# A decoder step on one core: w_in read with eight neighbouring rows per partition

## The chip, the cores and the metric

The kernel runs on one NeuronCore of a Trainium2 chip. Its engines work side by side: TensorE (matrix products, and transposes as products with an identity), VectorE, ScalarE, GpSimd, and SyncE, which mainly issues DMA transfers. The core's 16 DMA engines move data between the memory outside (DRAM) and the on-chip memory SBUF, which has 128 partitions. Products are written to PSUM and evacuated from there by ScalarE and VectorE. The metric is the device time of one execution in microseconds; lower is better.

## What is computed

One layer of a hybrid recurrent decoder for 2048 prompt tokens and 64 sample tokens, width 1024. The part that matters here is its beginning: the normalised input is multiplied by one wide matrix, and the product is cut into the inputs of all branches.

```python
IN_SPLITS = (LRU_WIDTH, LRU_WIDTH, GDN_QKV_W, GDN_VAL_W, GDN_HEADS, GDN_HEADS, D_MODEL, D_MODEL)
IN_WIDTH = sum(IN_SPLITS)                      # 8208
...
u = rms_norm(x, norm_pre)                      # x * rsqrt(mean(x*x) + eps) * norm_pre
z = jnp.einsum('btd,de->bte', u, w_in)         # w_in is (1024, 8208), float32
lru_x, lru_gate, gdn_qkv, gdn_gate, gdn_b, gdn_a, m_lru, m_gdn = jnp.split(z, offsets, axis=-1)
```

Behind it follow causal convolutions, a gated linear recurrence, a gated delta rule in chunks with its triangular inverses, two branch projections (w_br_lru, w_br_gdn), a gated merge and the output product (w_out). The sum over d in the product above has 1024 terms; in which order they are taken changes nothing but rounding.

## The kernel before

The prompt is worked through in four blocks of 512 tokens (`blkno` 0 to 3); block 1 also carries the 64 sample tokens. The contraction index of an input product has 1024 values; it is dealt out as eight tiles of 128 partitions. Both operands must have the same deal: partition p of tile k holds row k * 128 + p of w_in, and the transposed input holds the same index there.

**Weights.** `worder` is the list of all weight tiles in the order in which the products need them. In block 0 `wraw_of` loads a raw tile from DRAM through SyncE's queue: mostly 256 columns of w_in for all 1024 rows (1 MB; 128 columns in two cases), into `raw` of [128, 8, 256]. One row of w_in is 8208 floats or 32,832 bytes long, so each of the 1024 rows gives one contiguous piece of 1 KB. Tiles of the branch matrices are loaded by the same lines; their rows are 4 KB long. `split` then makes two tiles of it, high and low part (ScalarE writes the high part, GpSimd the low), in a buffer `whl` of which there are three. `wstore` writes both to DRAM (`dW`, 1 MB, contiguous); a buffer is free again when its store has landed and its products are done. From block 1 on `wfetch` reads `dW` back and w_in is not touched any more.

**Input.** `u_load` brings x into `ux` tiles (tokens on partitions), `u_norm` scales each token, and `u_tile(xh, k)` transposes the columns of tile k on TensorE (four tokens' tiles into one PSUM bank, five in block 1), where ScalarE and VectorE write high and low part, scaled by `npre[:, k]`, the norm's gains for the 128 rows of tile k. In a transpose the input tile is what TensorE loads as weights and the identity is what streams past. Block 0 does all eight tiles at the start; for the other blocks they are done during the output product of the block before. `npre` itself is loaded as eight rows of 128 (`r0`), transposed on TensorE and copied by VectorE.

**Order.** TensorE's order is that of the program; a small scheduler (`Weave`) interleaves side tasks between the products by estimated times. The other engines' orders come from the tile framework. All loads of weights, their stores and most other transfers go through SyncE's queue.

Of the kernel before, what the change touches and what calls it, by code (L numbers as in the profile page):

```python
# [22 lines left out]
F32 = mybir.dt.float32  # L23
# [47 lines left out]
C_LRUX, C_LRUG, C_Q, C_K, C_V, C_GG, C_B, C_ML, C_MG = 0, 1024, 2048, 3072, 4096, 5120, 6144, 6160, 7184  # L71
# [83 lines left out]
def body(ctx, tc, x_prompt, x_sample, state_lru_conv, state_lru_h, state_gdn_conv, state_gdn_S,  # L155
# [5 lines left out]
    V, T, SP = nc.vector, nc.tensor, nc.sync  # L161
    A, G = Ordered(tc, nc.scalar), nc.gpsimd

    win = w_in[0]
# [15 lines left out]
    def act(out, in_, func=AF.Copy, **kw):  # L180
        A.activation(out, in_, func, **kw)

    def gtile():
        t = pg.tile([128, 512], F32, name="g", tag="g")
        return t
# [8 lines left out]
    def tr(out, in_, idn):  # L194
        T.transpose(out, in_, idn)  # L195
        W.pe(TR)
# [33 lines left out]
    dW = [dram.tile([128, 2, 1024], F32, name=f"dW{i}") for i in range(len(wplace))]  # L230
    wstored, wstores, wraws = set(), [], {}

    def wraw_of(n):

        e = worder[n]
        if key(e) not in wraws:
            src, c = e
            if isinstance(c, tuple):
                raw = rp.tile([128, 4, 256], F32, name="raw", tag="raw")
                SP.dma_start(raw, src[c[1] * 512:(c[1] + 1) * 512, c[0] * 256:(c[0] + 1) * 256]  # L240
                             .rearrange("(k p) c -> p k c", p=128))
                wraws[key(e)] = raw
            else:
                two = [key(x) for x in worder[n:n + 7]].count((src.tensor.name, c + 128))
                w = 128 + 128 * two
                raw = rp.tile([128, 8, w], F32, name="raw", tag="raw")
                SP.dma_start(raw, src[:, c:c + w].rearrange("(k p) c -> p k c", p=128))
                for j in range(1 + two):
                    wraws[src.tensor.name, c + 128 * j] = raw[:, :, 128 * j:128 * j + 128]
        return wraws[key(e)]  # L250
# [44 lines left out]
    ident = const.tile([128, 128], F32, name="ident")  # L295
# [11 lines left out]
    npre = const.tile([128, 8], F32, name="npre")  # L307

    def u_load(bn, pool):
        nt = NCH + (1 if bn == SB else 0)  # L310
        xh = []
        for i in range(nt):
            m = 128 if i < NCH else NS
            xt = pool.tile([128, D], F32, name=f"ux{i}")
            SP.dma_start(xt[:m], xp[bn * TB + i * 128: bn * TB + (i + 1) * 128] if i < NCH else xs)
            xh.append((xt, m))
        return xh
# [14 lines left out]
    def u_tile(xh, k):  # L332
        hi = pA.tile([128, TB + NS], F32R, name="a", tag="a")
        lo = pA.tile([128, TB + NS], F32R, name="a", tag="a")
        for gi, grp in enumerate([xh[:4]] + ([xh[4:]] if len(xh) > 4 else [])):
            t = gtile()
            n = 0
            for xt, m in grp:
                tr(t[:, n:n + m], xt[:m, k * 128:(k + 1) * 128], ident[:m, :m])
                n += m  # L340
            cs = slice(gi * 512, gi * 512 + n)
            act(hi[:, cs], t[:, :n], AF.Copy, scale=npre[:, k:k + 1])
            V.scalar_tensor_tensor(out=lo[:, cs], in0=t[:, :n], scalar=npre[:, k:k + 1],
                                   in1=hi[:, cs].bitcast(F32), op0=OP.mult, op1=OP.subtract)
        return hi, lo
# [45 lines left out]
    with tc.tile_pool(name="init", bufs=2, side="right") as ip:  # L391
        rows = lambda a: a.rearrange("o (g p) -> (o g) p", p=128)
        with tc.tile_pool(name="u0", bufs=1) as up:
            r0 = ip.tile([8, 128], F32, name="r0")
            SP.dma_start(r0, rows(norm_pre))
            xh = u_load(0, up)
            t = gtile()
            tr(t[:, :8], r0, ident[:8, :8])
            V.tensor_copy(npre, t[:, :8])
            wraw = ip.tile([128, 8, 16], F32, name="wraw", bufs=1)  # L400
            SP.dma_start(wraw, win[:, C_B:C_B + 16].rearrange("(k p) c -> p k c", p=128))
            u_norm(xh, up)
            zz = ip.tile([128, 96], F32, name="zz", bufs=1)
            V.memset(zz, 0.0)
            V.tensor_copy(wst[:, 256:352], zz)
            V.tensor_copy(wst3[:, :, 0:16], wraw)
            V.tensor_tensor(out=wst3[:, :, 16:32], in0=wraw, in1=wst3[:, :, 0:16].bitcast(F32), op=OP.subtract)
            wfetch(2)
            r1 = ip.tile([128, 128], F32, name="r1")
            SP.dma_start(r1[8:40], lru_conv_w[0].rearrange("w (g p) -> (w g) p", p=128))  # L410
            SP.dma_start(r1[40:48], rows(lru_conv_b))
            SP.dma_start(r1[48:56], rows(lru_ba))
            SP.dma_start(r1[56:64], rows(lru_bx))
            SP.dma_start(r1[64:72], rows(lru_a_logit))
            SP.dma_start(r1[72:73], gdn_norm_w)
            SP.dma_start(r1[0:8], rows(norm_pre))
            r2 = ip.tile([128, 128], F32, name="r2")
            SP.dma_start(r2[:96], gdn_conv_w[0].rearrange("w (g p) -> (w g) p", p=128))
            SP.dma_start(dtb, bass.AP(tensor=gdn_dt_bias.tensor, offset=gdn_dt_bias.offset, ap=[[0, 128], [1, 8]]))
            SP.dma_start(negA, bass.AP(tensor=gdn_A_log.tensor, offset=gdn_A_log.offset, ap=[[0, 128], [1, 8]]))  # L420
            u = [u_tile(xh, k) for k in range(8)]
            t = gtile()
            tr(t[:, :73], r1[:73], ident[:73, :73])
            V.tensor_copy(par, t[:, :73])
        G.affine_select(out=tri, in_=ones, pattern=[[1, 128]], compare_op=OP.is_ge, fill=0.0,
                        base=0, channel_multiplier=-1)
        G.affine_select(out=offm.rearrange("p (a b) -> p a b", b=32), in_=ones.rearrange("p (a b) -> p a b", b=32),
                        pattern=[[-32, 4], [0, 32]], compare_op=OP.is_ge, fill=0.0, base=-32,
                        channel_multiplier=1)
        V.tensor_scalar(offm, offm, -1.0, None, op0=OP.mult)  # L430

        blk = const.tile([64, 64], F32, name="blk")
        blk3 = blk.rearrange("p (a b) -> p a b", b=8)
        G.affine_select(out=blk3, in_=ones[:64, :64].rearrange("p (a b) -> p a b", b=8),
                        pattern=[[-8, 8], [0, 8]], compare_op=OP.is_ge, fill=0.0, base=0, channel_multiplier=1)
        G.affine_select(out=blk3, in_=blk3, pattern=[[8, 8], [0, 8]], compare_op=OP.is_ge, fill=0.0,
                        base=7, channel_multiplier=-1)
        tris = const.tile([64, 64], F32, name="tris")
        V.tensor_tensor(out=tris, in0=blk, in1=tri[:64, :64], op=OP.mult)
        negs = const.tile([64, 64], F32, name="negs")  # L440
        V.tensor_scalar(negs, tris, 1.0, BIG, op0=OP.subtract, op1=OP.mult)
        bsel = blk3[:, :, 0]
        G.memset(halog, 0.0)
        G.memset(halol, 0.0)
        G.memset(hlast, 0.0)
        t = gtile()
        tr(t[:, :96], r2[:96], ident[:96, :96])
        V.tensor_copy(cwg.rearrange("p w g -> p (w g)"), t[:, :96])
        V.tensor_scalar(hba, par[:, 48:64], 0.5, None, op0=OP.mult)
        lp = ip.tile([128, 8], F32, name="lp")  # L450
        log1pexp_neg_abs(ip, lp, lal, [128, 8])
        V.scalar_tensor_tensor(out=ls4[:, 0:8], in0=lal, scalar=0.0, in1=lp, op0=OP.min, op1=OP.subtract)
        V.tensor_scalar(ls4[:, 0:8], ls4[:, 0:8], 4.0, None, op0=OP.mult)
        V.tensor_scalar(ls4[:, 8:16], ls4[:, 0:8], -1.0, None, op0=OP.mult)
        tc.keep_in_program_order(A.activation(negA, negA, AF.Exp))
        V.tensor_scalar(negA, negA, -1.0, None, op0=OP.mult)
# [52 lines left out]
    for blkno in range(NBLK):  # L509
# [402 lines left out]
        for g in range(8):  # L912
# [3 lines left out]
            raw = kl.tile([128, 2, 128], F32, name="gwr", tag="er", bufs=2)  # L916
# [324 lines left out]
        for q in range(4):  # L1241
# [11 lines left out]
            for i, k in order:  # L1253
                c0, m = ntok[i]
                r0 = 128 - m
# [19 lines left out]
        for i, (c0, m) in enumerate(ntok):  # L1275
            r0 = 128 - m
# [42 lines left out]
```

## Time and profile before

| | |
|---|---|
| Median of three runs | 2709.49 us (2701.82 to 2710.34) |
| Profiled execution | 2704.15 us, its span 2702.4 us |
| TensorE busy | 2576.4 us (95% of the span) |
| VectorE, ScalarE, GpSimd busy | 56%, 33%, 21% |
| Queue of SyncE and ScalarE (q1) | 295162 packets, 553.57 MB, 65.1% of 16 engines' span |
| Issues of w_in loads | 31 of 1024 KB, 2 of 512 KB |
| Mean granted clock of TensorE | 0.984 |

A share of the span is an average over stages with different limits. The rows below therefore cut block 0 (about the first 700 us) into stages. A window of the DMA view says how many packets began in it, how many MB they moved, and what share of the 16 engines' time in the window they took; share times 16 times the window's length, divided by packets, is the mean time of one packet.

### The profile page before, as it was taken

To read this page: it belongs to the slowest core of one execution; us is meant where nothing else is said; L and a number is where in the kernel's file an instruction comes from. 1 tells how busy PE (TensorE), PEld (TensorE's weight loads), DVE (VectorE), ACT (ScalarE), POOL (GpSimd) and SP (SyncE) were. 2 spreads that over 40 slices of the span, in tenths; PEclk is the share of its full clock that TensorE was granted. 3 is DMA by queue.
4 is the path that set the end of the run, shared out by engine and by line. 5 is a ranking of instruction groups with operands and counts; after the bars stand their busy time and mean duration, and the time that the engine had idled before them with its cause. 6 is when DMAs were issued, how large, how long until landed. Compare 5 with 4: busy or idle time off the path is not lost.

```text
span 2702.4 us, 39930 instructions
## 1 busy us (share of the span) xinstructions
PE 2576.4 (95%) x15332; PEld 2234.1 (83%) x15332; DVE 1515.1 (56%) x3449; ACT 880.1 (33%) x1708; POOL 561.2 (21%) x444
## 2 busy tenths in 40 slices
PE   7777898889999999999999999999999999999999
PEld 5656677778899999998999788888889788888888
DVE  4557677753455767777423557566523457566522
ACT  4225533332432452333203225333302235333301
POOL 3433522336212011000210211100110111110200
PEclk9898899999999999999999999999999999999999
DMA  8998976878877656544465787554467786655465
GB/s 241 262 271 193 270 226 166 178 235 316 304 249 255 193 180 193 162 154 134 171 216 219 252 271 227 199 175 156 156 241 257 252 280 215 206 170 168 160 238 199
DMA packets 309177, 581.82 MB, mean 215 GB/s; under 512 B 70561, under 2 KB 218042, under 8 KB 263930
## 3 DMA queue, kind: packets, MB, share of 16 engines
q1 hardware_dynamic: 295162, 553.57, 65.1%
q10 hardware_dynamic: 13824, 25.70, 2.5%
q8 instruction: 121, 1.98, 0.3%
q14 instruction: 70, 0.57, 0.1%
HBM read 421.61 MB, written 157.59 MB: 214 GB/s over the span
## 4 chain that ended last, share of the span: by engine, by line
PE 78%; DMA 7%; DVE 6%; issue 3%; ACT 2%; POOL 2%; SPq 1%; ACTq 0%; POOLq 0%; DVEq 0%
PE mm L533 19%; PE mm L531 18%; PE mm L529 18%; PE g L191 8%; PE c L191 5%; DMA dW<-whl 3%; PE g L195 3%; DVE cvy L560 2%; PE mm L1264 2%; PE mm L1266 2%; PE mm L1262 2%; DMA er<-dgc 1%; POOL whl L204 1%; DMA dgc<-gr 1%; DMA raw<-in_w_in_dram 1%
## 5 line engine op out<-in xcount | busy, mean ns | idle before, releaser
L533 PE MATMUL mm<-a,whl 128*128 128x512 f32 (+2 forms) x2288 | 840.3, 367 | 11.4 <-POOL whl L204 11.4
L529 PE MATMUL mm<-a,whl 128*128 128x512 f32 (+2 forms) x2288 | 835.4, 365 | 13.6 <-ACT whl L143 6.4
L531 PE MATMUL mm<-a,whl 128*128 128x512 f32 (+2 forms) x2288 | 835.6, 365 | 0.0
L533 PEld LDWEIGHTS mm<-a,whl 128*128 128x128 f32 x2288 | 436.9, 191 | 70.7 <-POOL whl L204 14.1
L529 PEld LDWEIGHTS mm<-a,whl 128*128 128x128 f32 x2288 | 436.8, 191 | 69.5 <-ACT whl L143 7.6
L531 PEld LDWEIGHTS mm<-a,whl 128*128 128x128 f32 x2288 | 436.2, 191 | 51.8
L560 DVE SCALAR_TENSOR_TENSOR cvy<-cvr,cwg,cvy 128x512 f32<-128x512 f32 x288 | 263.2, 914 | 19.1 <-ACT cvy L143 13.5
L204 POOL TENSOR_TENSOR whl<-raw,whl 128x1024 fp32r<-128x1024 f32 x80 | 200.4, 2507 | 255.9 <-ACT whl L143 243.8
L533 PE MATMUL mm<-a,whx 128*128 128x512 f32 (+2 forms) x592 | 210.1, 355 | 0.0
L531 PE MATMUL mm<-a,whx 128*128 128x512 f32 (+2 forms) x592 | 209.6, 354 | 0.0
L529 PE MATMUL mm<-a,whx 128*128 128x512 f32 (+2 forms) x592 | 208.3, 352 | 0.0
L1200 DVE SCALAR_TENSOR_TENSOR pt<-tm,mm 128x512 f32<-128x512 f32 (+1 forms) x80 | 47.3, 593 | 188.7 <-PE mm L533 188.7
L143 ACT ACTIVATE cvr<-mm 128x512 f32<-128x512 f32 (+1 forms) x160 | 81.6, 510 | 185.2 <-PE mm L533 178.7
L143 ACT ACTIVATE whl<-raw 128x1024 fp32r<-128x1024 f32 x88 | 93.0, 1057 | 146.9 <-DMA dW<-whl 88.6
L1055 POOL TENSOR_TENSOR st<-st,mhalf 128x4 f32<-128x4 f32 x32 | 32.2, 1007 | 513.8 <-DVE st L1053 383.8
L143 ACT ACTIVATE th<-cvy 128x512 f32<-128x512 f32 (+1 forms) x96 | 61.9, 645 | 203.6 <-DVE cvy L560 158.3
L1266 PE MATMUL mm<-whl,bt 128*128 128x256 f32 x440 | 123.8, 281 | 0.8 <-DVE yss L1240 0.8
L1262 PE MATMUL mm<-whl,bt 128*128 128x256 f32 x440 | 123.9, 282 | 0.2 <-ACT bt L143 0.2
L1264 PE MATMUL mm<-whl,bt 128*128 128x256 f32 x440 | 124.0, 282 | 0.0
L533 PEld LDWEIGHTS mm<-a,whx 128*128 128x128 f32 x592 | 112.0, 189 | 13.8 <-issue 1.5
L529 PEld LDWEIGHTS mm<-a,whx 128*128 128x128 f32 x592 | 111.8, 189 | 12.0
L531 PEld LDWEIGHTS mm<-a,whx 128*128 128x128 f32 x592 | 111.7, 189 | 11.9
(328 smaller groups left out, 4511.2 us busy)
## 6 DMA issues: line engine op xcount, KB each, us to landing
whl<-dW SPq DMA_DIRECT2D x199, 1024.0 KB
dW<-whl SPq DMA_DIRECT2D x88, 1024.0 KB
whx<-dW SPq DMA_DIRECT2D x65, 1024.0 KB
raw<-in_w_in_dram SPq DMA_DIRECT2D x31, 1024.0 KB
dtm<-tmo ACTq DMA_DIRECT2D x48, 256.0 KB
tm<-dtm SPq DMA_DIRECT2D x48, 256.0 KB
ux<-in_x_prompt_dram SPq DMA_DIRECT2D x16, 512.0 KB
er<-dgc SPq DMA_DIRECT2D x32, 256.0 KB
```

The lines of the kernel that those rows point to most:

```text
L143: r = f(*args, **kw)
L191: T.matmul(out, a, b, start=start, stop=stop)
L195: T.transpose(out, in_, idn)
L204: (eng or G).tensor_tensor(out=lo, in0=src, in1=hi.bitcast(F32), op=OP.subtract)
L529: T.matmul(ps[:, :n], wh, mh[:, c0:c0 + n], start=k == 0, stop=False)
L531: T.matmul(ps[:, :n], wh, ml[:, c0:c0 + n], start=False, stop=False)
L533: T.matmul(ps[:, :n], lo[:, k, :], mh[:, c0:c0 + n], start=False, stop=k == 7)
L560: V.scalar_tensor_tensor(out=y[:, :TB], in0=raw[:, i:i + TB], scalar=cw[:, i, ti:ti + 1], in1=y[:, :TB], op0=OP.mult, op1=OP.add)
L1200: proj(mov, lambda ps, c0, n: V.scalar_tensor_tensor(out=t_[:, c0:c0 + n], in0=x[:, c0:c0 + n], scalar=1.0, in1=ps[:, :n], op0=OP.add, op1 ...
L1262: T.matmul(ps[:, :256], mh[:, cs], wh[:, k % 4], start=k == 0, stop=False)
L1264: T.matmul(ps[:, :256], mh[:, cs], wl[:, k % 4], start=False, stop=False)
L1266: T.matmul(ps[:, :256], ml[:, cs], wh[:, k % 4], start=False, stop=k == 7)
```

## The change

Partition p of an input product now holds rows 8p to 8p + 7 of w_in, and tile k is the k-th of each eight. Three places follow it: the loads of w_in (`krows`, used by `wraw_of` for tiles of w_in alone and by the small gate load `wraw`), the transposes of the input, which take every eighth column of x, and `npre`, which in this deal is a plain reshape of norm_pre and is loaded directly.

```diff
+    def krows(a, by8):
+
+        return a.rearrange("(p k) c -> p k c", k=8) if by8 else a.rearrange("(k p) c -> p k c", p=128)
+
     def wraw_of(n):
...
-                SP.dma_start(raw, src[:, c:c + w].rearrange("(k p) c -> p k c", p=128))
+                SP.dma_start(raw, krows(src[:, c:c + w], src is win))
...
-                tr(t[:, n:n + m], xt[:m, k * 128:(k + 1) * 128], ident[:m, :m])
+                tr(t[:, n:n + m], xt[:m].rearrange("t (p k) -> t k p", k=8)[:, k], ident[:m, :m])
...
-            r0 = ip.tile([8, 128], F32, name="r0")
-            SP.dma_start(r0, rows(norm_pre))
+            SP.dma_start(npre, norm_pre.rearrange("o (p k) -> (o p) k", k=8))
             xh = u_load(0, up)
-            t = gtile()
-            tr(t[:, :8], r0, ident[:8, :8])
-            V.tensor_copy(npre, t[:, :8])
             wraw = ip.tile([128, 8, 16], F32, name="wraw", bufs=1)
-            SP.dma_start(wraw, win[:, C_B:C_B + 16].rearrange("(k p) c -> p k c", p=128))
+            SP.dma_start(wraw, krows(win[:, C_B:C_B + 16], True))
```

The order of instructions changes at the start alone. TensorE's first instructions before (r is the tile r0, ux a tile of x, g a PSUM bank):

```order
L195 MATMUL g<-ident,r_208 128x8
L195 MATMUL g<-ident,ux_210 128x128
L195 MATMUL g<-ident,ux_212 128x128
L195 MATMUL g<-ident,ux_214 128x128
L195 MATMUL g<-ident,ux_216 128x128
```

and now:

```order
L195 MATMUL g<-ident,ux_209 128x128
L195 MATMUL g<-ident,ux_211 128x128
L195 MATMUL g<-ident,ux_213 128x128
L195 MATMUL g<-ident,ux_215 128x128
L195 MATMUL g<-ident,ux_209 128x128
```

The transpose of r0 is gone (and with it VectorE's copy into npre); the rest follows in the same order. SyncE's queue begins before with these transfers:

```order
L395 DMA r_208<-in_norm_pre_dram 8x128
L315 DMA ux_210<-in_x_prompt_dram 128x1024
L315 DMA ux_212<-in_x_prompt_dram 128x1024
L315 DMA ux_214<-in_x_prompt_dram 128x1024
L315 DMA ux_216<-in_x_prompt_dram 128x1024
L401 DMA wraw<-in_w_in_dram 128x8x16
L247 DMA raw<-in_w_in_dram 128x8x256 x2
```

and now:

```order
L398 DMA npre<-in_norm_pre_dram 128x8
L319 DMA ux_209<-in_x_prompt_dram 128x1024
L319 DMA ux_211<-in_x_prompt_dram 128x1024
L319 DMA ux_213<-in_x_prompt_dram 128x1024
L319 DMA ux_215<-in_x_prompt_dram 128x1024
L401 DMA wraw<-in_w_in_dram 128x8x16
L251 DMA raw<-in_w_in_dram 128x8x256 x2
```

The first transfer goes to all 128 partitions; nothing else moved in the queue, here or later.

## Rows read from the trace of the kernel before

**Rows 1.** Page, 40 slices of the span: DMA engines' busy share in tenths.
```profile
DMA  8998976878877656544465787554467786655465
```
**Rows 2.** Windows: stretch, us, busy (instructions) by engine, PEclk, DMA share, GB/s.
```profile
96.00:360.00 264.00, 209.69 (x866) 165.62 (x865) 164.49 (x270) 103.50 (x148) 108.63 (x64) 0.89 0.93 246
360.00:600.00 240.00, 215.19 (x1258) 175.71 (x1257) 170.12 (x303) 83.42 (x158) 74.70 (x38) 0.97 0.73 192
600.00:690.00 90.00, 89.46 (x394) 72.80 (x393) 33.91 (x32) 27.91 (x36) 58.80 (x31) 1.00 0.86 310
```
**Rows 3.** Chain of waits from 30 to 360 us, longest pieces: start, us, what.
```profile
96.77 17.89 DMA dW<-whl
123.79 7.22 DMA dW<-whl
146.28 9.44 DMA er<-dgc
178.31 9.85 DMA dW<-whl
256.93 21.65 DMA dW<-whl
...
314.33 17.17 DMA dW<-whl
```
**Rows 4.** Timeline of SyncE's queue: start, us of the issue, line, transfer.
```profile
95.46 1.21 SPq L247 DMA_DIRECT2D raw<-in_w_in_dram  x1
...
246.94 0.43 SPq L247 DMA_DIRECT2D raw<-in_w_in_dram  x1
...
298.15 1.00 SPq L247 DMA_DIRECT2D raw<-in_w_in_dram  x1
```
**Rows 5.** DMA view, 516 to 519 us (stores alone): packets, MB, share of 16 engines.
```profile
q1 hardware_dynamic: 127, 1.04, 83.9%
```
**Rows 6.** DMA view, 602 to 605.4 us: a load of w_br.
```profile
q1 hardware_dynamic: 1055, 1.06, 92.4%
```
**Rows 7.** DMA view, 464.3 to 476.6 us: a load of w_in.
```profile
q1 hardware_dynamic: 1063, 1.26, 101.6%
```
**Rows 8.** DMA view, 397.6 to 404.7 us: a load of w_in.
```profile
q1 hardware_dynamic: 1107, 1.62, 94.0%
```
**Rows 9.** DMA view, 98.1 to 110.5 us: a load of w_in.
```profile
q1 hardware_dynamic: 1156, 1.52, 102.4%
```
**Rows 10.** DMA view, 212 to 226 us: a load of w_in.
```profile
q1 hardware_dynamic: 1371, 2.28, 99.5%
```
**Rows 11.** DMA view, 250 to 260 us: most of a load of w_in.
```profile
q1 hardware_dynamic: 819, 0.90, 98.3%
```
**Rows 12.** DMA view, issues from 30 to 360 us: count, KB each.
```profile
raw<-in_w_in_dram SPq DMA_DIRECT2D x19, 1024.0 KB
```
**Rows 13.** Chain of waits from 360 to 600 us, shares by line.
```profile
by line: issue 21.3%; DVE cvy L560 12.9%; PE c L191 9.3%; PE g L191 7.5%; POOL whl L204 7.0%; PE mm L533 6.2%; PE mm L531 5.5%; PE mm L529 5.2%; ACT cvy L143 3.2%; PE g L195 2.9%; POOL st L1055 2.5%; ACT whl L143 2.4%; DVE R L977 2.0%; DVE 
```
**Rows 14.** Timeline of ScalarE at the start: start, us, instruction [idle before <-releaser].
```profile
19.09 1.06 ACT L143 ACTIVATE whl<-raw 128x1024 fp32r<-128x1024 f32 x1 [3.59 <-DMA raw<-in_w_in_dram]
20.05 1.83 ACT L143 ACTIVATE a<-g,npre 128x512 fp32r<-128x512 f32 x3
```
**Rows 15.** Instructions on the ux tiles: count, ns min/median/max, first and last start, forms.
```profile
L195 PEld LDWEIGHTS g<-ident,ux x136: 134/141/231, 7.7 to 2069.9; 128*128 128x128 f32 x128, 64*128 64x128 f32 x8
L195 PE MATMUL g<-ident,ux x136: 243/272/477, 7.7 to 2070.0; 128*128 128x128 f32 x128, 64*128 64x64 f32 x8
...
L330 DVE TENSOR_SCALAR ux<-ux,urr x9: 746/753/764, 6.8 to 2052.5; 128x1024 f32<-128x1024 f32 x8, 64x1024 f32<-64x1024 f32 x1
```
**Rows 16.** The same view of line 797, a copy with permuted axes.
```profile
L797 DVE COPY invTT<-invT x4: 1119/1134/1141, 236.9 to 2265.2; 128x1024 f32<-128x1024 f32 x4
```
**Rows 17.** DMA view, 11.7 to 15.3 us: the first load of w_in.
```profile
q1 hardware_dynamic: 1144, 1.05, 91.7%
```

## The prediction, written before the result

> **What bounds the kernel now.** I read the page's slices first: the DMA engines are nearly full in the first slices, about 0.8 to 0.9 busy through slice 7, and looser after that [rows 1]. The change touches the loads of w_in, and these are issued in block 0 alone (later blocks read the split copies back from dW). So I cut block 0 into stages [rows 2]. [...] From 360 to 600 the DMA share is 0.73, and from 600 to 690 TensorE is full (89.46 of 90 us, clock 1.00). Only the first of the three is a stage where DMA decides.
>
> The chain of waits says the same [rows 3]. Between 30 and 360 us its longest pieces are stores of split weights (dW<-whl) and one broadcast (er<-dgc): 17.89, 7.22, 9.44, 9.85, 21.65 and 17.17 us, together 83.2 us. A store of 1 MB that has the DMA engines to itself takes 3 us [rows 5], so these wait in the queue. What is ahead of them stands in SyncE's list [rows 4]: some microseconds before each of the six pieces a load of w_in was issued (before the first at 95.46 us, before the fifth at 246.94, before the last at 298.15). A store must land before its whl buffer is free (three of them), and ScalarE's next split waits for that.
>
> **The price of a w_in load.** I take windows filled by one load and turn the share of 16 engines into time per packet. A load of 1 MB is 1024 packets of 1 KB (1.05 MB). Pure stores: 0.839 x 16 x 3 us = 40.3 us for 1.04 MB, 38.7 us per MB [rows 5]. A load of w_br, which has the same shape but rows 4 KB apart: 0.924 x 16 x 3.4 = 50.3 us for 1055 packets, 48 ns each [rows 6]. A w_in load alone at 464 us: 1.016 x 16 x 12.3 = 199.9 us, less 0.21 MB of stores (8.1), is 192 us for 1024 packets, 187 ns each [rows 7]. Another at 397 us: 106.8 less 0.57 MB (22.1) is 84.7 us, 83 ns each [rows 8]. So w_in's packets cost two to four times w_br's, at the same size, beside the same kind of stores. The difference is where the rows lie: w_in's rows are 8208 x 4 = 32,832 bytes apart, and in the order "(k p)" the eight pieces of a partition are 128 rows, 4.2 MB, apart.
>
> I call loads near 187 ns costly. Three more are at 98 us (203.2 less 18.2 for 0.47 MB, 181 ns) [rows 9], at 212 us (222.9 less 47.6 for 1.23 MB, 171 ns) [rows 10] and at 250 us (157.3 us for 819 packets, 192 ns) [rows 11]. Of the 19 full loads from 30 to 360 us [rows 12] these three are costly, and the other 16 I put at the 83 ns of [rows 8].
>
> **The change, part by part.**
>
> *The loads of w_in (the main term).* Same number of packets, same 1 KB. The eight pieces of a partition now are neighbouring rows, 32,832 bytes apart, and a partition starts 262,656 bytes after the one before. No row of the trace shows this pattern. The lower bound of its price is w_br's 49 ns (rounded up), the upper the 187 ns of the costly loads. I take 55 ns, near the lower end: w_br's regular step from row to row is fast, and the costly pattern is the one whose consecutive pieces jump by megabytes. Then a costly load gives back (187 - 55) x 1024 / 16 ns = 8.4 us of all engines, another (83 - 55) x 64 ns = 1.8 us, and all from 30 to 360 us 3 x 8.4 + 16 x 1.8 = 54 us (62 at 49 ns).
>
> How much lies on the path? At least what the chain shows: the pieces at 96.77 and 256.93 stand behind a costly load (2 x 8.4), the other four behind one of the rest (4 x 1.8): 24 us. At most all 54 (or 62), because at a share of 0.93 each transfer queues behind the one before. TensorE then limits: its 209.69 busy us in 264, less what the clock of 0.89 cost, leave room for at least 54 us. Once it is fed, VectorE's and GpSimd's work between the products stands next in the chain, so I don't take all: 42. After 360 us I take nothing: DMA is 0.73 busy there and the chain names VectorE, TensorE and "issue" but neither raw nor dW [rows 13].
>
> *The start.* ScalarE idles 3.59 us for the first raw tile at 19.09 us, with the evacuations of the input's transposes queued behind it; the next one begins at 20.05 [rows 14]. A faster load gives 0 to 3.6; I take 2.
>
> *npre.* Gone: one transpose and one copy, both in idle time at the start. New: SyncE's first DMA has 128 pieces of 32 bytes, not 8 of 512. Its first reader is ScalarE's evacuation at 20.05 us, and it is the first DMA of the kernel; behind it in SyncE's queue stand the loads of x, which could start a fraction of a microsecond later. Cost 0; without that cover it would be one small DMA's latency. The small load wraw keeps its 1024 pieces and is first read by products that come after all transposes.
>
> *The transposes.* Their input is read with a step of 8 elements, by the weight load. Now the load takes 141 ns (median of 136) under a matmul of 272 ns [rows 15], so it may grow to 272 ns for nothing. The nearest strided rows are VectorE's: a permuted copy of 128x1024 takes 1134 ns, a plain pass over as many elements 753 [rows 15, 16], a factor of 1.5, or 212 ns here. Cost 0 in a row of transposes, some 0.1 us at the first of each group; I take 1 us in all. The order of instructions on every engine is otherwise the same, so no new wait arises.
>
> Sum: 2704.15 - 42 - 2 + 1 = 2661 us against the profiled execution (span 2702.4). The three runs have a median of 2709.49, 5.3 above that execution, and spread over 8.5 us; the median of the changed kernel should stand between 2661 and 2666. I give 2663.
>
> **The rivals.**
>
> *Nothing changes.* The same 1024 rows are read in another order. If some columns of w_in simply lie badly (all on few parts of the memory), the order can't help: 2704 to 2709 us. For it: the load at 464 us is costly from end to end, while the first load, with the same order of rows, ran at 0.917 x 16 x 3.6 = 52.8 us for 1144 packets, 46 ns [rows 17]; so columns matter. Against it: that a pattern with the same rows can reach 46 ns also shows that these rows are not costly by themselves. [...] Chance 0.17.
>
> *Slower: the new order collides.* All 16 DMA engines now walk neighbouring rows, and if they meet on the same part of the memory, every load runs at the 187 ns of [rows 7]. The 16 others from 30 to 360 us then cost (187 - 83) x 64 = 6.7 us more each, 107 us; with the same part on the path as above (42 of 54) 83 us, and some 10 after 360 us: 2797 us. It decides from a mean of (3 x 187 + 16 x 83) / 19 = 99 ns per packet of w_in. Against it: w_br's loads walk rows at a regular step too and don't collide. Chance 0.11.
>
> *The strided transposes set the pace.* [...] Chance 0.06.
>
> **How the numbers follow.** A measurement of this kernel tells 0.3% (8 us) from no change. Forecast 0.66, its own range 2636 (62 + 3.6 us) to 2690 (half of the excess stays and little of it is on the path). Nothing changes 0.17 and strided transposes 0.06 end within 0.3%; slower 0.11. So faster 0.66, same 0.23, slower 0.11. The range for 8 in 10 leaves out the collision and little else: 2634 to 2714.
>
> **What would show it.** Right: the window of a w_in load shows above 250 GB/s when alone; waits of ScalarE's split for dW<-whl (pieces of 17 to 22 us) are gone from the chain; the windows of 96 to 360 us finish 40 us earlier with a granted clock near 1; blocks 1 to 3 take as long as before. Wrong: w_in packets still at 80 ns or more; weight loads of the ux transposes over 272 ns; or the loads fast, and block 0 as long as before because VectorE or TensorE ends last, which would make the share on the path the step that failed.

## The result, and the profile after

The changed kernel takes 2688.7 us (median of 5 runs, 2683.3 to 2696.5), the kernel before 2702.0 us (5 runs, 2701.4 to 2710.3) measured beside it. The ratio of the runs is 0.9938 (95% interval 0.9918 to 0.9958), 0.6% less; the medians lie 13.3 us or 0.5% apart. That is faster, clear of the noise, as forecast, and inside the range, but the forecast of 2663 was a gain of 41 us on the profiled execution, which took 2704.15; the changed kernel's profiled execution took 2688.70 (span 2687.0), 15.5 less. The mechanism is there at about a third of its size.

The busy share of the DMA engines in the 40 slices looks almost as before [rows 1]; in the first fourteen slices, which hold block 0 and what follows it, some stand a tenth lower and some a tenth higher:

```profile
DMA  8999976769787655554465896555466786555465
```

In the windows of [rows 2] (stretch, busy us of each engine with its instructions, granted clock, DMA share, GB/s), the first stage does 257 GB/s, not 246, and TensorE has 9 us more work in it; its DMA share is still 0.91 and its clock 0.91:

```profile
96.00:360.00 264.00, 218.57 (x951) 173.30 (x949) 174.95 (x286) 108.71 (x158) 107.86 (x64) 0.91 0.91 257
360.00:600.00 240.00, 215.80 (x1210) 177.02 (x1211) 163.69 (x286) 84.21 (x158) 79.29 (x43) 0.94 0.70 187
600.00:690.00 90.00, 89.48 (x394) 72.88 (x393) 33.12 (x32) 26.36 (x33) 52.34 (x30) 1.00 0.91 326
```

The long pieces of the chain from 30 to 360 us (start, us, what) are still stores of split weights, at most 18.3 us where [rows 3] has one of 21.65, and otherwise of the same size:

```profile
91.62 18.34 DMA dW<-whl
...
138.15 9.70 DMA dW<-whl
...
236.07 18.30 DMA dW<-whl
...
258.01 16.61 DMA dW<-whl
...
281.43 15.08 DMA dW<-whl
```

Why they stand is in the DMA view of the windows of three loads (packets, MB, share of 16 engines), at 92.9 to 105.2, 446.1 to 458.1 and 381.3 to 387.2 us. They are the loads of [rows 9], [rows 7] and [rows 8]:

```profile
q1 hardware_dynamic: 1165, 1.53, 103.2%
...
q1 hardware_dynamic: 1080, 1.41, 98.5%
...
q1 hardware_dynamic: 1079, 1.38, 98.4%
```

By the prediction's arithmetic (share x 16 x the window, less 38.7 us for each MB beyond the load's 1.05): 203.1 - 18.6 = 184.5 us, **180 ns** a packet; 189.1 - 13.9 = 175.2, **171 ns**; 92.9 - 12.8 = 80.1, **78 ns**. Before they were 181, 187 and 83. The costly loads are as costly as they were, the ordinary ones a little cheaper.

What ScalarE waited for between 30 and 360 us shows the gain directly (us in total, times, longest). The kernel before:

```profile
ACT whl L143 <- DMA dW<-whl: 88.6, 16, 13.7
```

The changed kernel:

```profile
ACT whl L143 <- DMA dW<-whl: 69.0, 15, 11.3
```

The 41st split of a weight, a good place to read the lead at the end of that stage, starts at 353.22 us in the kernel before,

```profile
353.22 1.05 ACT L143 ACTIVATE whl<-raw 128x1024 fp32r<-128x1024 f32 x1
```

and in the changed kernel at 336.31 us, 16.9 us sooner for 19.6 us less of that wait:

```profile
336.31 1.05 ACT L143 ACTIVATE whl<-raw 128x1024 fp32r<-128x1024 f32 x1
```

### The profile page after: what moved, and what is told of

Its sections match the earlier page's. It is cut to its first block, busy times and chain, and to the rows that moved or that the text cites. A ratio compares the mean times of both kernels' runs of the same rounds, so it can differ in the third digit from the quotient of the medians.

```text
span 2687.0 us, 39927 instructions
## 1 busy us (share of the span) xinstructions
PE 2577.7 (96%) x15331; PEld 2237.3 (83%) x15331; DVE 1514.9 (56%) x3448; ACT 881.1 (33%) x1708; POOL 560.1 (21%) x444
## 3 DMA queue, kind: packets, MB, share of 16 engines
q10 hardware_dynamic: 13824, 25.70, 2.6%
## 4 chain that ended last, share of the span: by engine, by line
PE 79%; DVE 7%; DMA 6%; issue 3%; ACT 2%; POOL 2%; SPq 1%; ACTq 0%; POOLq 0%; DVEq 0%
PE mm L533 19%; PE mm L531 19%; PE mm L529 19%; PE g L191 8%; PE c L191 5%; DMA dW<-whl 3%; DVE cvy L560 3%; PE g L195 3%; PE mm L1264 2%; PE mm L1266 2%; PE mm L1262 2%; POOL whl L204 1%; DMA raw<-in_w_in_dram 1%; PE mm L191 1%; DVE invt L792 1%
## 5 line engine op out<-in xcount | busy, mean ns | idle before, releaser
L560 DVE SCALAR_TENSOR_TENSOR cvy<-cvr,cwg,cvy 128x512 f32<-128x512 f32 x288 | 266.3, 925 | 19.5 <-ACT cvy L143 13.9
```

The lines of the kernel that those rows point to most:

```text
L560: V.scalar_tensor_tensor(out=y[:, :TB], in0=raw[:, i:i + TB], scalar=cw[:, i, ti:ti + 1], in1=y[:, :TB], op0=OP.mult, op1=OP.add)
```

## The experiments

Each kernel ran beside the kernel before on the same chip (median there 2699.6, 2702.5, 2700.3 and 2700.4 us in the four groups of runs). Three figures are worked out for each from its trace. "Loads" is the DMA time of loads 4 to 22, those between 30 and 360 us: the recorded times of their 1 KB packets, summed, over 16 engines. "Wait" is the wait of ScalarE's splits for dW<-whl from 30 to 360 us, as above. "Lead" is how much sooner than 353.22 us the 41st split starts. These three come from one execution of each kernel. The times of one kernel's executions lie 3 to 18 us apart, so a few us of lead tell nothing.

| kernel | loads, us | wait, us | lead, us | median, us | ratio to before, interval |
|---|---|---|---|---|---|
| before | 125.5 | 88.6 | 0 | 2702.0 | 1 |
| changed | 113.2 | 69.0 | 16.9 | 2688.7 | 0.9938 (0.9918 to 0.9958) |
| loads only | 113.2 | 65.7 | 15.6 | 2689.8 | 0.9953 (0.9933 to 0.9974) |
| transposes only | 123.1 | 80.5 | 0.7 | 2704.8 | 1.0014 (1.0000 to 1.0027) |
| 4 KB pitch | 70.3 | 39.6 | 32.2 | 2674.2 | 0.9904 (0.9885 to 0.9922) |
| no costly columns | 96.1 | 48.6 | 30.6 | 2673.8 | 0.9898 (0.9883 to 0.9913) |
| old order, no costly columns | 105.7 | 73.6 | 17.0 | 2688.3 | 0.9951 (0.9938 to 0.9964) |
| third deal | 120.1 | 70.1 | 10.6 | 2689.4 | 0.9957 (0.9942 to 0.9972) |
| costly loads on ScalarE's queue | 114.9 | 24.4 | 16.1 | 2685.9 | 0.9941 (0.9922 to 0.9959) |
| all loads on ScalarE's queue | 106.4 | 0.4 | 21.8 | 2668.2 | 0.9878 (0.9860 to 0.9897) |
| all but two on ScalarE's queue | 107.6 | 0 | 25.2 | 2668.9 | 0.9882 (0.9861 to 0.9903) |
| old order, the same queues | 120.3 | 1.4 | 10.8 | 2689.1 | 0.9956 (0.9937 to 0.9975) |
| the same queues, no costly columns | 90.3 | 0 | 28.5 | 2663.0 | 0.9858 (0.9840 to 0.9876) |
| the same queues, 4 KB pitch | 64.9 | 0 | 35.2 | 2659.9 | 0.9852 (0.9835 to 0.9868) |

### The two halves of the change

The first kernel has the new loads alone: it is the changed kernel with its transposes put back as they were, as below, and npre loaded and transposed by the old lines:

```
- tr(..., xt[:m].rearrange("t (p k) -> t k p", k=8)[:, k], ...)
+ tr(..., xt[:m, k * 128:(k + 1) * 128], ...)
```

> Only the loads of w_in are dealt out anew; the transposes and npre stay as before, so the products pair rows with the wrong columns of x (the work and its amount are the same). Theory 'loads': the whole gain comes from the loads, which now keep the DMA engines busy some 13 us less from 30 to 360 us; this kernel is then 1 to 3 us faster than the changed one (2683 to 2689 us), since its transposes read contiguously. Theory 'elsewhere' (start, npre, another alignment of the side tasks): it stays at the time of the kernel before, 2700 to 2705 us.

The second has the new transposes and npre with the old loads.

> Only the transposes and npre are changed; w_in is loaded in the old deal (rows are paired wrongly, the amount of work is the same). Theory 'loads': 0 to 3 us slower than before, 2702 to 2706 us, with weight loads of the ux transposes at 193 ns instead of 141 under matmuls of 277 instead of 272. Theory 'elsewhere': as fast as the changed kernel, about 2688 us.

Measured: 2689.8 and 2704.8 us. The loads alone give what the whole change gives, within the noise, and the transposes with npre cost between nothing and 7 us. The changed kernel, which has them and is not behind the first (2688.7), suggests that their cost is nearer to nothing; the runs don't tell 3 us from none. The strided weight load has a price, though. In the changed kernel the instructions on the ux tiles (count, ns min/median/max) answer to [rows 15]:

```profile
L195 PEld LDWEIGHTS g<-ident,ux x136: 182/193/231, 7.7 to 2054.8; 128*128 128x128 f32 x128, 64*128 64x128 f32 x8
L195 PE MATMUL g<-ident,ux x136: 272/277/479, 7.7 to 2054.9; 128*128 128x128 f32 x128, 64*128 64x64 f32 x8
```

141 ns have become 193, a factor of 1.37 and still under the matmul's 277. In the pace of the transposes little of it arrives: four of one group, which overlap, take 0.61 us at 696.40 us, and took 0.60 at 709.05 us in the kernel before. Behind 600 us the transposes of a group start 113 ns apart (median), where it was 109.

### What sets a packet's price: pitch or columns

Both the next kernels are the changed kernel with other addresses in the loads. The first reads the same packets from rows 4 KB apart:

```
- SP.dma_start(raw, krows(src[:, c:c + w], src is win))
+ d = c if c < C_B else c - 16
+ flat = w_in[0].rearrange("a b -> (a b)")[:8192 * 1024].rearrange("(r c) -> r c", c=1024)
+ part = flat[d // 1024 * 1024:d // 1024 * 1024 + 1024, d % 1024:d % 1024 + w]
+ SP.dma_start(raw, krows(part, True))
```

> The changed kernel, but the loads of w_in read the same number of 1 KB pieces from rows 4 KB apart (w_in seen as a flat array cut into rows of 1024), so the weights are other numbers of w_in. Theory 'addresses' (the price of a w_in packet is set by the pitch of 32,832 bytes): all loads run at 48 to 50 ns per packet, 3.1 to 3.5 us each, and the DMA engines are relieved of some 55 us from 30 to 360 us. If those are on the path as fully as the change's 13 us were, the kernel takes 2635 to 2645 us. Rival 'path': another engine takes over after the first 15 us, 2665 to 2680 us. Rival 'mix': the price comes from the stores beside the loads, then packets stay near 80 ns and the time at 2688.

The second reads 256 columns earlier where a load would be costly. In the changed kernel's trace that is where a load starts at column 768 of a block of 1024 (the blocks behind the 16 gate columns begin 16 columns later, hence the c - 16). These seven loads average 127 to 180 ns a packet by its records, the other 24 full loads 51 to 113:

```
+ cc = c - 256 if src is win and (c if c < C_B else c - 16) % 1024 == 768 else c
```

> The changed kernel, but the seven loads whose columns begin at 768 modulo 1024 read the columns 256 before them instead (wrong weights, same amount). Theory 'columns': those loads fall from 170 to 180 ns per packet to 75 to 90, 6 us each; the three of them before 360 us lie on the path, the four after it mostly not: 2668 to 2675 us. Rival 'position': the loads at these positions are dear because of what runs beside them, then they keep 170 ns and the time stays at 2688.

With the 4 KB pitch the load at 365.7 to 371.7 us, which was an ordinary one, shows in the DMA view

```profile
q1 hardware_dynamic: 1106, 1.59, 92.2%
```

or 88.5 - 20.9 = 67.6 us, 66 ns a packet; the mean over the 19 loads is 70.3 x 16,000 / 19,456 = 58 ns. So near 55 ns is to be had for these packets, but by another layout of the rows; none of the orders tried here reached it. The edit changes two things at once: the rows lie 4 KB apart and not 32, and the 1024 pieces of a load then lie within 4.2 MB and not 33.6. No run parts the two. In the second kernel the load that was costly at 446 us now lies at 434.0 to 440.7,

```profile
q1 hardware_dynamic: 1088, 1.45, 97.0%
```

which is 104.0 - 15.5 = 88.5 us, 86 ns instead of 171, at the same place of the program. The price goes with the columns, not with the place.

The times say something on the other step. The 4 KB pitch saves 55 us of DMA time from 30 to 360 us, the second kernel 29 us, and both end at 2674, some 26 us under the kernel before. In the chain of the first, from 30 to 360 us, the stores have fallen from 26.9% (changed kernel, first line) to 6.4% (second line), and VectorE, "issue" and TensorE stand in their place:

```profile
by line: DMA dW<-whl 26.9%; DVE cvy L560 12.6%; issue 7.1%; DVE invt L792 4.5%; PE mm L533 4.2%; PE mm L529 4.0%; PE mm L531 3.9%; DVE invT L794 3.8%; POOL whl L204 2.9%; PE g L191 2.3%; DVE lru L880 1.8%; DVE Mt L749 1.7%; ACT whl L143 1.6
...
by line: DVE cvy L566 10.0%; issue 9.1%; PE mm L539 9.1%; PE mm L535 9.0%; PE mm L537 8.7%; DMA dW<-whl 6.4%; PE g L191 5.1%; DVE invt L798 3.8%; DVE invT L800 3.2%; DMA er<-dgc 3.2%; POOL whl L204 2.6%; DVE lru L886 1.9%; DVE Mt L755 1.7%;
```

### Order and columns apart, and a scan of the columns

The kernel before with its old order, and the same line for cc:

> The kernel before (old row order, old transposes), with one edit: the seven costly loads of w_in (first column 768 in a block of 1024) read the 256 columns before theirs; so the columns of the products that use them are wrong, nothing else. It takes the costly columns away without the new order. Theory 'two parts': the order is worth some 13 us on the ordinary loads, the columns another 13, and they add up; this kernel then ends 11 to 15 us under the kernel before, near the changed kernel, its costly loads at 80 to 100 ns a packet and the ordinary ones still at 83 to 110. Rival 'one relief': the three costly loads before 360 us alone set the end, and the order is worth nothing without them; then this kernel ends 22 to 28 us under the kernel before, as the changed kernel without costly columns does.

Measured 2688.3 us, 14 under the kernel before; its lead is 17.0 us. So the costly columns alone are worth about as much as the new order alone, and the two add up (14 and 13, against the 26 of the kernel with both).

The packet records of loads 4 to 22 also say where the order's gain lies. Sorted by first column in a block of 1024 (0, 256, 512, 768), the mean packet takes 86, 101, 76 and 178 ns in the kernel before and 81, 74, 75 and 178 ns in the changed one. So most of the 12.3 us saved comes from the six loads that start at column 256: (101.3 - 74.2) x 6 x 1024 / 16 ns = 10.4 us. The two other kernels with the old order on SyncE's queue take 101 and 104 ns there (transposes only; old order without costly columns), the two others with the new order 75 and 78 (loads only; no costly columns). Why the order matters for these columns and hardly for the rest, no run here shows.

The scan:

```
+ cc = 512 + 32 * (len(wraws) // 2) if src is win else c     # the n-th load: 512 + 32 n
```

> The changed kernel, but the n-th load of w_in (n from 0) reads 256 columns from column 512 + 32 n on instead of its own; all products of w_in are wrong, nothing else. One look at the price of a packet by its first column. Theory 'columns': the loads near n = 8 (column 768) cost 150 ns a packet and more, whatever their place in time, and the price falls on both sides, to 50 to 90 ns at 128 or more columns away; so at the places of the costly loads in time (93, 202, 239 us) there is nothing special. Rival 'read for the first time': the loads that were cheap in the run without costly columns were so because the same columns had been read a moment ago; then nearly all loads here, which overlap their predecessors by seven eighths, are cheap, near 50 to 80 ns, with no peak.

The scan ran once, so its time (2708.9 us) isn't compared. The DMA view of three of its loads, at 96.5 to 103.3 us (first column 704), 171.1 to 185.4 (832) and 282.4 to 294.0 (992):

```profile
q1 hardware_dynamic: 1120, 1.47, 103.3%
...
q1 hardware_dynamic: 1211, 1.57, 98.3%
...
q1 hardware_dynamic: 1689, 3.61, 79.5%
```

That is 112.4 - 16.3 = 96.1 us, 94 ns; 224.9 - 20.1 = 204.8 us, 200 ns; and 147.6 - 99.1 = 48.5 us, 47 ns. Between them the mean times of the packets run, from column 736 on in steps of 32: 108, 160, 178, 199, 180, 162, 152, 107, 46, 77 ns. There is a peak of six steps, its top at column 832, though every load overlaps the one before by seven eighths. The rival of the repeated read falls. Why these columns, no run here shows; column 992, just behind them, is the cheapest of the scan.

A third deal of the rows, with the same columns:

```
+ SP.dma_start(raw, src[:, c:c + w].rearrange("(i k e) c -> e i k c", k=8, e=16))
```

> The changed kernel, but the loads of w_in (not the transposes) use a third deal of the 1024 rows: partition 8 e + i takes, as its k-th piece, row 16 (8 i + k) + e, so that pieces of one partition lie 16 rows (525,312 bytes) apart and pieces of the partitions 8 apart are neighbouring rows; the products of w_in mix wrong rows, nothing else. Same columns, same packets. Theory 'columns': the price follows the columns and the set of rows, not the deal; costly loads 140 to 190 ns, the others 70 to 100, time 2685 to 2697. Rival 'meeting': the old and the new deal both let the engines meet on the same parts of the memory, and a deal without that brings the packets to 50 to 60 ns: 2671 to 2680, as with a pitch of 4 KB.

Its costly load at 452.4 to 463.7 us:

```profile
q1 hardware_dynamic: 1064, 1.27, 101.8%
```

184.1 - 8.5 = 175.6 us, 171 ns. The ordinary loads average 85 ns (89 before, 77 in the changed kernel). So none of three deals of the same 1024 rows touches the costly loads, and they move the others by 12 ns on average at most (those at column 256 take 86 ns in the third). The time, 2689.4, is that of the changed kernel.

### The loads on another queue

These kernels leave the addresses as they are and issue loads of w_in on ScalarE's queue, so that stores no longer stand behind them in SyncE's. The table ahead of the prediction calls q1 the queue of SyncE and ScalarE, but it is SyncE's alone. In the kernel before, ScalarE's own issues (80 of 256 KB and 16 of 288 KB) add up to 25.69 MB, and q10 moves 25.70; and with all loads of w_in issued on ScalarE, a load shows in q10 (1054 packets and 1.06 MB of it from 440 to 454 us). First the seven costly ones alone, as below, then all (far is then src is win):

```
+ far = src is win and (c if c < C_B else c - 16) % 1024 == 768
+ (nc.scalar if far else SP).dma_start(raw, krows(src[:, c:c + w], src is win))
```

> The changed kernel, with the seven costly loads issued on ScalarE's DMA queue and all else on SyncE's; the result is the same. Theory 'ring': a store of split weights waits 17 to 18 us in the chain because it stands in one queue behind the costly load; from another queue the engines take packets of both in turn, the store lands after some 6 us, three pieces of 17 us shrink by about 10 each, part of it on the path: 2672 to 2682 us, 8 to 16 under the changed kernel. Rival 'engines': the 16 engines are held by the costly packets from whichever queue they come, 12 us of them must pass before or beside the store: 2686 to 2691, as the changed kernel. Second rival 'ScalarE waits': the issue waits on ScalarE for the raw buffer to come free and holds up the splits and evacuations behind it: 2695 or more.

> The changed kernel, with all loads of w_in issued on ScalarE's DMA queue, stores and the rest on SyncE's; the result is the same. 'Ring': stores no longer stand behind any load of w_in, 2668 to 2680 us. 'Engines': 2686 to 2691. 'ScalarE waits': the 33 issues each may wait on ScalarE for a raw buffer, 2695 or more, and the chain from 30 to 360 us shows ScalarE waiting for raw buffers.

The first came out at 2685.9 us: the number of "engines", though the stores did pass the loads (the wait for them fell from 69.0 to 24.4 us):

```profile
ACT whl L143 <- DMA dW<-whl: 24.4, 7, 6.1
```

The wait has moved to the costly loads themselves and to what SyncE's queue holds. In its chain from 30 to 360 us:

```profile
104.97 11.23 DMA raw<-in_w_in_dram
...
212.04 15.56 DMA raw<-in_w_in_dram
...
233.17 14.57 DMA raw<-in_w_in_dram
```

With all loads moved, the kernel took 2668.2 us, 20.5 under the changed kernel, a time that "ring" had forecast. Only 0.4 us of waits for dW<-whl are left:

```profile
ACT whl L143 <- DMA dW<-whl: 0.4, 1, 0.4
```

That these waits were what cost the time is not shown. Of the gain over the changed kernel 4.9 us (21.8 - 16.9) are there at the 41st split. The rest comes after 360 us. The 65th split starts at 588.37 us in the changed kernel,

```profile
588.37 1.05 ACT L143 ACTIVATE whl<-raw 128x1024 fp32r<-128x1024 f32 x1
```

and at 567.23 with all loads on ScalarE's queue:

```profile
567.23 1.05 ACT L143 ACTIVATE whl<-raw 128x1024 fp32r<-128x1024 f32 x1
```

The lead over the changed kernel has grown to 21.1 us in a stage from which the prediction took nothing [rows 13]. Some 5 us of that are what the changed kernel's own execution lost there (below). What shrinks in the chain of this stage is "issue", from 18.8% in the changed kernel to 9.9%, and not a wait for stores; why, no run shows. Its window in the second of these kernels shows 7.7 us more work of TensorE than in the changed one, at a granted clock of 0.99:

```profile
360.00:600.00 240.00, 223.45 (x1281) 181.53 (x1280) 163.83 (x288) 89.02 (x163) 97.05 (x52) 0.99 0.73 205
```

Its early splits were late, though (the fifth starts at 55.21 us, not 43.71). The next kernel was to mend that by leaving the first two loads on SyncE's queue:

```
+ far = src is win and len(wraws) >= 4
```

> The changed kernel, with the first two loads of w_in on SyncE's queue as they were and all later ones on ScalarE's; the result is the same. With all loads on ScalarE's queue the kernel took 2668.2 us, but the first splits came 10 to 16 us late (the fifth split at 55.2 us, not 43.7), since the first load ran ahead of the input's. Theory 'late start': the lateness at the start is part of the end, so keeping the first two in their place gives most of it back: 2655 to 2662 us. Rival 'slack': the lateness was taken up by 360 us by other waits, and the time stays at 2665 to 2671. The stores (dW<-whl) as waits of ScalarE's splits from 30 to 360 us, 69.0 us in the changed kernel, should be near nothing in either case.

It took 2668.9 us, but its fifth split still starts at 54.98 us, so the edit did not take the lateness away, and what the lateness costs is open.

With the same queues, the old order, then no costly columns, then the 4 KB pitch:

> The kernel before (old row order, transposes and npre), with the first two loads of w_in on SyncE's queue and all later ones on ScalarE's; the result is the same. It asks what the new row order is worth once stores don't stand behind loads. Theory 'the queue was the path': a packet's price mattered by way of the stores queued behind it, so the order is worth little now, 0 to 5 us: this kernel ends within 5 us of the same arrangement in the new order. Rival 'the engines are the path': the DMA engines are still full, and the order keeps its 13 to 17 us.

> The changed kernel with the first two loads on SyncE's queue and the rest on ScalarE's, and with the seven costly loads reading the 256 columns before theirs (the products of these columns are wrong). It asks what the costly columns are worth once stores don't stand behind loads. Theory 'the queue was the path': 0 to 5 us under the same arrangement with its own columns. Rival 'the engines are the path': the costly loads' 6 us each, three before 360 us, still count, 10 to 18 us under it.

> The kernel of the 4 KB pitch (loads of w_in in 1 KB pieces from rows 4 KB apart; the products of w_in are wrong), with the first two loads on SyncE's queue and the rest on ScalarE's. It asks how much of the time cheap packets and a free queue can give together. The 4 KB pitch alone took 2674.2, the queue alone 2668.9, the queue without costly columns 2663.0. Theory 'floor': behind the DMA stand VectorE's, GpSimd's and TensorE's own work, and block 0 can't get more than a few us shorter: 2658 to 2665. Rival 'no floor yet': DMA time still sets the end, and the 58 us of engine time that the cheaper packets save (173.6 to 115.4) give another 15 us or more: 2648 to 2654.

Measured: 2689.1, 2663.0 and 2659.9 us. The new order is worth 20.2 us here (2689.1 to 2668.9), by the intervals some 12 to 28 us, so at least about the 13 it was worth on SyncE's queue: "the queue was the path" falls for the order. The costly columns are worth 5.9 us (15 on SyncE's queue), just above the 0 to 5 of the first theory, and the intervals of the two runs overlap; this one stays open. And with cheap packets and a free queue the kernel ends at 2660, as "floor" said. From 30 to 360 us its TensorE is busy 295 of 330 us:

```profile
30.00:360.00 330.00, 295.25 (x1354) 237.69 (x1353) 228.16 (x424) 147.27 (x224) 151.91 (x90) 0.97 0.83 275
```

The version to keep is the changed kernel with the loads of w_in on ScalarE's queue: 2668 us, 1.2% under the kernel before, which neither the order nor the queue gives alone (2689 each).

## Why the prediction was right in direction and wrong in size

**The step that failed is the price of a packet in the new order, 55 ns.** It was put "near the lower end" because w_br's steps are regular and "the costly pattern is the one whose consecutive pieces jump by megabytes". The four loads that the prediction called costly measured 171 to 180 ns in the new order (171 to 187 in the old; three more after 460 us 127 to 150, where the old order had 136 to 157). The 16 others from 30 to 360 us took 77 on average (89 in the old, not the 83 of the one load of [rows 8]). The DMA time saved from 30 to 360 us is therefore 125.5 - 113.2 = 12.3 us, not 54. The bounds, 49 and 187, did hold both; the choice between them rested on a reason that the rows had already spoken against. All loads before had the same megabyte jumps, and they ranged from 51 ns (the load of [rows 17]; the prediction's 46 counts 120 smaller packets in) to 187 ns [rows 7]. What differs between loads of one pattern can't be made by the pattern alone. That left the columns, as "Nothing changes" said, and it deserved the larger chance: for the costly loads it was simply true.

With 12.3 us in place of 54, and the same share of 42 in 54 on the path, the prediction's sum is 2704.15 - 9.6 - 2 + 1 = 2693.6 us, against 2688.70 in the profiled execution: the price alone makes nearly all of the miss.

**The share on the path, 42 of 54, was off as well, but it did little here.** The runs give the curve: saving 12.3 us of DMA time led to 16.9 us at the 41st split, 5.4 to 10.6 (third deal), 19.8 to 17.0, 29.4 to 30.6, and 55.2 to only 32.2. So up to 30 us each us saved gives 0.9 to 2 us of lead (and the waits for stores fall by 0.9 to 1.7 us for each us of lead), and behind them other work decides. For a saving of 12 us the share was too small, for 54 too large. Had the packets really come down to 55 ns, the kernel would by that curve have come to about 2674, the 4 KB pitch's time, and not to 2663. The prediction named that floor (VectorE's and GpSimd's work between the products), and it took 12 us off for it where some 22 were due at the 41st split.

**The start.** Taken 2, found about 1: ScalarE's idle time before the first split fell from 3.59 [rows 14] to 2.46 us, and the split starts 1.07 us sooner. The reason given, a faster load, did not come true: by the packet records the first load took 51 ns a packet before and 52 after, and it began 0.7 us sooner (11.0 us, not 11.7). ScalarE's timeline of the changed kernel:

```profile
18.02 1.06 ACT L143 ACTIVATE whl<-raw 128x1024 fp32r<-128x1024 f32 x1 [2.46 <-DMA raw<-in_w_in_dram]
18.98 1.83 ACT L143 ACTIVATE a<-g,npre 128x512 fp32r<-128x512 f32 x3
```

**npre and the transposes.** The estimate for the strided weight load was 212 ns, hidden up to 272; it measured 193. That 272 is a limit is not shown: it is the time of one matmul, while the transposes of a group start 109 ns apart, and the longest weight load of a ux tile took 231 ns in either kernel. The 1 us taken for them is within the 0 to 7 that the run of this half allows.

**After 360 us.** Taken 0. In the profiled executions 4.9 us of the lead are given back: the 65th split starts at 588.37 us after, and before at

```profile
600.37 1.05 ACT L143 ACTIVATE whl<-raw 128x1024 fp32r<-128x1024 f32 x1
```

The granted clock of that stage is 0.97 before and 0.94 after (by the clock's records 13.7 and 27.3 of its 240 us at the lower level, a granted share of 0.50); TensorE is busy 215 and 216 us of it, for 1258 and 1210 matmuls. The kernel with the 4 KB pitch, also at 0.94, gave back 5.1 us; those with the new loads alone (0.98) and without costly columns (0.97) gave nothing back. So the loss goes with the lower clock. Whether other executions of the changed kernel have it too isn't settled. From the end of block 0 the lead stays (12.0 us at 600 us, 15.4 in the span); that the later blocks take some 3 us less, where 0 was said, rests on one execution of each.

**Of the rivals,** none is the whole answer. The collision did not show: no load is dearer in the new order than the dearest in the old. The strided transposes did not set the pace: their weight load took 193 ns, under the 272 named in the prediction, and the transposes of a group start 113 ns apart where it was 109. "Nothing changes" was right in its reason for 7 of the 31 full loads and left out that the others gain 12 ns on average from 30 to 360 us.

**The range** held the time, but not for its reason. Its upper end stood for half of the excess staying; in fact the costly loads kept all of it and the gain came from a few ordinary ones, and 2688.7 lies inside the forecast's own 2636 to 2690 by 1.3 us, which is luck. The chances went the right way; the likeliest case was too far from the next one. One reading was loose: slices 6 and 7 of [rows 1] stand at 0.7 and 0.6, not at 0.8 to 0.9, but the stage rests on the windows of [rows 2], which are right.

## What to carry to other kernels

When loads of one pattern differ nearly fourfold in price, as here from 51 to 187 ns a packet, the pattern alone isn't the cause: sort them by what does differ (here the first column) before you price a new pattern, and take the price in the new one from the same columns. Saved transfer time reached the end here only until other engines' work stood there: read the wait that it would remove (here 88.6 us of ScalarE's splits for stores) and what stands behind it, and allow for a second half that gives much less than the first (here 29.4 us saved gave a lead of 30.6 us, and 55.2 us one of 32.2). Try bulk loads on another engine's queue than the stores that free buffers: moving all but the first two was worth 11 us in the old order and 20 in the new. Don't take the vanished wait for the gain, though: moving only the dearest loads took 44.6 us off the wait for stores and was worth 3 us, which the measurement can't tell from nothing.

## What the runs showed of the hardware

- Loads of 1 KB pieces from rows 32,832 bytes apart took from 46 to 200 ns a packet, depending mostly on the first column: in the scan 160 at column 768, 199 at 832, 152 at 928 and 46 at 992. Three deals of the same rows left the costly ones before 360 us at 167 to 184 ns, while the loads that start at column 256 took 101, 74 and 86 ns in them. From rows 4096 bytes apart, and so within 4.2 MB, packets of the same size took 58 ns on average over loads 4 to 22.
- The weight load of a transpose that reads every eighth fp32 element took 193 ns (median of 136), against 141 for neighbouring elements, a factor of 1.37; the matmul went from 272 to 277.
- With all but the first two on ScalarE's queue, the same loads took less of the engines' time than from SyncE's: 107.6 us instead of 113.2 for loads 4 to 22 in the new order, 120.3 instead of 125.5 in the old. The costly loads at 93 and 202 us fell from 180 and 176 to 146 and 151 ns there, the one at 239 us only from 180 to 178. With only the seven costly loads moved there was no such saving (114.9 us). No run separates why.
